# Seven-product weight sums with other signs, and two of them made by one 1024-column instruction

## The chip, the cores and the metric

The kernel runs on one core of a Trainium2 chip. The core has TensorE (matmuls; the profile lists its weight loads apart, as PEld), VectorE (DVE), ScalarE (ACT), GpSimd (POOL) and SyncE (SP), which here issues the loads and stores. The metric is the device time of one execution in microseconds (us); several executions are made, and their median is given.

## The reference, cut to what matters

One layer of a block on 256 tokens of width 4096, in float32:

```python
xn = rms_norm(h, norm_in_g[i])
proj = xn @ w_in[i]
q, k, v, z_a, a_c, g_c, z_c = split(proj)
y_a = chunked_attention(q, k, v, rel_table[i])
y_a = rms_norm(y_a, attn_out_g[i]) * silu(z_a)
y_c = conv_module(a_c, g_c, ...)
y_c = rms_norm(y_c, conv_out_g[i]) * silu(z_c)
h = h + concatenate([y_a, y_c]) @ w_out[i]
gate = sigmoid(rms_norm(h, ple_norm_g[i]) @ w_ple_gate[i] + b_ple_gate[i])
h = h + gate * (p[i] @ w_ple[i])
return rms_norm(h, final_g)
```

Nearly all of the work is products of 256 rows with large weight matrices: `w_in` (4096 x 14336), `w_out` and `w_ple_gate` (4096 x 4096 each), `w_pw` (2048 x 2048) and `w_ple` (256 x 4096).

## The kernel before

**Products in parts.** Each float32 operand is split into a high part (a cast to the matmul's rounded float32) and a low part (the operand less the high part). A product then takes three matmuls: high by high, low by high and high by low. ScalarE casts a weight tile `wt` to its high part `wh` (`prepare`, line 304), VectorE subtracts it to get the low part `wl` (`minus`, line 321). A weight tile is 128 rows by 1024 columns (512 KB), loaded by SyncE's queue.

**Seven products for eight.** Most of the large products run as `mixed_product`. It makes a 2 x 2 arrangement of output blocks, two halves h of 128 tokens by two groups j of 512 columns, each in a PSUM bank of its own. It walks over pairs of 128-row blocks of the weights. A pair has four weight blocks w00, w01 (first row block, column group 0 and 1, in the tile `w0`) and w10, w11 (second row block, in the tile `w1`). A plain pair takes eight block products, 24 matmuls. A seven-product pair takes seven, 21 matmuls, in Strassen's manner: P1 to P7, some of them with sums of the token blocks (`s_of`, made ahead) and with sums of the weight blocks. P1, P5, P6 and P7 add up in four extra PSUM banks (`acc_P` in the profile). After the last seven-product pair `on_helpers` adds these to the blocks (`helper_sums`). The orders in which plain and seven-product pairs follow each other are written out by hand (`steady`, `dense`, `delayed`, `early`, `late`; a star marks a seven-product pair; `early` has six). There are 117 such pairs in the kernel.

**What a seven-product pair does around its matmuls.** The high parts `h0` (w00 alone) and `h1` (w10, w11) are there already when the pair begins, since `prepare` makes them a unit ahead. VectorE then makes, in this order: the low part `l0` of w00 (512 columns, line 321); the sum w00 + w01 into the first half of `w0` (line 324); the low part `l1` of w10 and w11 (1024 columns, line 321); w01 + w11 into the second half of `w0`; then w00 + w01 + w11 into the second half of `w1` and that plus w10 into its first half. ScalarE casts the two sums in `w0` to `ah` (line 486) and the two in `w1` to `bh` (line 489). Then follow `prepare` for the next unit, work from the queue `later` (`fill`), and VectorE's low parts `al` and `bl` (line 321). The matmuls (line 446) use `h0`, `l0` in P1, `h1`, `l1` in P2 and P3, `ah`, `al` in P5 and P7, `bh`, `bl` in P6 and P4, in the order P1, P2, P3, P5, P7, P6, P4.

**What sets the order.** The weights' casts, sums and low parts are chained: on each engine they keep the order in which the code makes them (`chain`). What is not chained (matmuls, block ends, transposes and their splits, the attention and the layer norm) is placed among them by the framework's scheduler when the program is built; each engine then runs its list in order. Five weight tiles and five tiles each of high and low parts go round, so the engines ahead of TensorE can lead it by a few units and no more.

**The stages**, in order of time: the first product and its transposes; four rounds of a gate/convolution product and a query/key product (both with seven-product pairs) and a value product (plain, line 255, `product`), with attention and the convolution's taps filled in between; a layer norm of the convolution's result; the product with `w_pw` (plain, from about 901 us); the products for the two output gates, with `w_out` and with `w_ple_gate` (all with seven-product pairs); two last column groups in plain products, and the closing norm.

Of the kernel before, what the change touches and what calls it, by code (L numbers as in the profile page):

```python
# [16 lines left out]
P = 128  # L17
NB = 512
# [13 lines left out]
def hybrid_block(  # L32
# [290 lines left out]
    def plus(out, a, b):  # L323
        return chain(nc.vector.tensor_tensor(out, a, b, ALU.add))  # L324

    def product(w, col, lhs, kblocks, pool=None, tag="acc", ahead=None, lag=(), begun=None, fills=2):

        acc = begun or [  # L330
            (pool or ps_acc).tile([P, NB], F32, tag=tag, name=f"acc{h}") for h in range(NH)
        ]
        starts = range(FIRST if begun else 0, kblocks, KC)
        kept = list(starts[len(starts) - len(lag) :]) if lag else []
        held = []
        for k0 in starts:
            kc = min(KC, kblocks - k0)
            keep = k0 in kept
            if lag:
                wh, wl = weight_parts(w, col, k0, kc, lag[kept.index(k0)] if keep else None)  # L340
            else:
                (wt,), (wh,) = take(w, col, None, k0, "one")
                wl = part("wl")
                minus(wl, wt, wh)
                prepare()
            if keep:
                held.append((k0, kc, wh, wl))
            for k in range(kc):
                for h in range(1 if keep else NH):
                    accumulate(acc[h], h, lhs, k0 + k, wh, wl, k, kblocks)  # L350
                if ahead and begun and k0 + k == FIRST:
                    ahead(k0)
            if ahead:
                ahead(k0 + kc)
            fill(fills)

        def rest():
            for k0, kc, wh, wl in held:
                for k in range(kc):
                    accumulate(acc[1], 1, lhs, k0 + k, wh, wl, k, kblocks)  # L360

        return (acc, rest) if lag else acc
# [63 lines left out]

    def mixed_product(
        w, col, lhs, comb, order, on_helpers, ahead=None, fills=0, on_begin=None, apart=NB
    ):

        c = [[ps_acc.tile([P, NB], F32, tag="acc", name=f"acc{h}{j}") for j in range(2)] for h in range(NH)]
        helper = {}
        begun, ends = set(), {}
        for n, (_, seven) in enumerate(order):
            for name in ("P1", "P5", "P6", "P7", "P2", "P3", "P4") if seven else ("P2", "P3", "P4", "X"):
                ends[name] = n
        banks = {"P2": c[0][0], "P3": c[0][1], "P4": c[1][0], "X": c[1][1]}
        made = []  # L440

        def add(name, x, w2, n, final):

            for kind, (a, b) in enumerate(((x[0], w2[0]), (x[1], w2[0]), (x[0], w2[1]))):
                made.append(
                    nc.tensor.matmul(  # L446
                        banks[name], a, b, start=name not in begun,
                        stop=final and ends[name] == n and kind == 2,
                    )
                )  # L450
                begun.add(name)

        def block(kb, h):
            t = lhs[kb // 4]
            return [t[:, kb % 4, q, h * P : (h + 1) * P] for q in range(2)]

        last_seven = max((n for n, (_, seven) in enumerate(order) if seven), default=None)
        for n, (pair, seven) in enumerate(order):
            if ahead:
                ahead(pair)  # L460
            (w0, w1), (h0, h1) = take(w, col, apart, pair, "seven" if seven else "pair")
            l0, l1 = part("wl"), part("wl")
            if not seven:
                for wt, wh, wl in ((w0, h0, l0), (w1, h1, l1)):
                    minus(wl, wt, wh)
                prepare()
                fill(fills[0] if isinstance(fills, tuple) else fills)
                parts = ((h0, l0), (h1, l1))
                places = [(k, j, h) for k in range(2) for j in range(2) for h in range(NH)]
                if n in (0, len(order) - 1):  # L470
                    places = [(k, j, h) for j in range(2) for h in range(NH) for k in range(2)]
                for k, j, h in places:
                    name = (("P2", "P3"), ("P4", "X"))[h][j]
                    add(name, block(2 * pair + k, h), [t[:, j] for t in parts[k]], n, k == 1)
                continue
            begins = not helper
            if begins:
                for name in ("P1", "P5", "P7", "P6"):
                    helper[name] = ps_tmp.tile([P, NB], F32, tag="tmp", name=f"acc_{name}")
                banks.update(helper)  # L480
            minus(l0[:, :1], w0[:, :1], h0[:, :1])
            plus(w0[:, 0], w0[:, 0], w0[:, 1])
            minus(l1, w1, h1)
            plus(w0[:, 1], w0[:, 1], w1[:, 1])
            ah, bh = part("wh"), part("wh")
            chain(nc.scalar.copy(ah, w0))  # L486
            plus(w1[:, 1], w0[:, 0], w1[:, 1])
            plus(w1[:, 0], w1[:, 1], w1[:, 0])
            chain(nc.scalar.copy(bh, w1))  # L489
            prepare()  # L490
            fill(fills[1] if isinstance(fills, tuple) else fills)
            al, bl = part("wl"), part("wl")
            minus(al, w0, ah)
            minus(bl, w1, bh)
            first = len(made)

            def s_of(i):
                t, at = comb[pair // 4], pair % 4
                return [t[:, at + i // 2, q, (i % 2) * P : (i % 2 + 1) * P] for q in range(2)]

            k0, k1 = 2 * pair, 2 * pair + 1
            add("P1", block(k0, 0), (h0[:, 0], l0[:, 0]), n, True)
            add("P2", block(k1, 0), (h1[:, 0], l1[:, 0]), n, True)
            add("P3", s_of(3), (h1[:, 1], l1[:, 1]), n, True)
            add("P5", s_of(1), (ah[:, 0], al[:, 0]), n, True)
            add("P7", s_of(0), (ah[:, 1], al[:, 1]), n, True)
            add("P6", s_of(2), (bh[:, 1], bl[:, 1]), n, True)
            add("P4", block(k1, 1), (bh[:, 0], bl[:, 0]), n, True)
            if begins and on_begin:
                on_begin()  # L510
            if begins:
                tc.add_manual_dep(
                    made[first].ins, last_transpose[0].ins.name,
                    mybir.DependencyInfo(mybir.DependencyClass.NoSync, mybir.DependencyReason.DATA),
                    reason="transposes before the helpers take their banks",
                )
            if n == last_seven:
                on_helpers(helper)
        return c
# [4 lines left out]
    def helper_sums(helper, z):  # L524


        nc.scalar.copy(z[1][0], helper["P1"])
        tt(z[1][0], helper["P6"], z[1][0], ALU.add)
        tt(z[0][1], helper["P5"], z[1][0], ALU.add)
        tt(z[1][0], helper["P7"], z[1][0], ALU.add)  # L530
        tt(z[1][1], helper["P5"], z[1][0], ALU.add)

    def sum_tiles():
# [4 lines left out]
    def scaled_pair(w, col, apart, order, r, fills):  # L538
# [11 lines left out]
        def finals():  # L550
            for h, j in QUARTERS:
                stt(
                    z[h][j], c[h][j], r[:, h : h + 1], z[h][j],
                    ALU.mult, ALU.subtract if j else ALU.add,
                )

        closing.append(finals)
# [480 lines left out]
    def gated(ys, c0, col, r_y, order):  # L1038
# [7 lines left out]
        acc = mixed_product(w_in0, col + c0 * NB, xT, xS, order, on_helpers, fills=2)  # L1046
        for h, j in QUARTERS:
            zz, y = z[h][j], ys[c0 + j][:, h, :]
            tt(zz, acc[h][j], zz, ALU.subtract if j else ALU.add)
            nc.scalar.activation(zz, zz, AF.Silu, scale=r_x[:, h : h + 1])  # L1050
            later.append(partial(stt, y, y, r_y[:, h : h + 1], zz, ALU.mult, ALU.mult))

# [16 lines left out]
    for c0 in range(0, D // NB, 2):  # L1069
# [8 lines left out]
        def on_helpers(helper):  # L1078
# [1 line left out]
            h00, h01, h10, h11 = (hs[c0 + j][:, h, :] for h in range(NH) for j in range(2))  # L1080
            tt(h00, helper["P1"], h00, ALU.add)
            helper_sums(helper, z)
            tt(h01, h01, z[0][1], ALU.subtract)
            tt(h10, h10, z[1][0], ALU.add)
            tt(h11, h11, z[1][1], ALU.subtract)

        acc = mixed_product(
            w_out0, c0 * NB, yT, yS, dense if c0 else late, on_helpers,
# [54 lines left out]
    def gated_pair(c0, order, ahead):  # L1143
# [7 lines left out]
        def on_helpers(helper):  # L1151
            stt(z[0][0], helper["P1"], r_h[:, :1], rows[0], ALU.mult, ALU.add)
            helper_sums(helper, z)
            for h, j in QUARTERS[1:]:
                zz = z[h][j]
                stt(
                    zz, zz, r_h[:, h : h + 1], rows[j],
                    ALU.mult, ALU.subtract if j else ALU.add,
                )
            fgs.extend(broadcast_row(final_g, (c0 + j) * NB, NB) for j in range(2))  # L1160

# [8 lines left out]
        todo = []  # L1170
        for h, j in QUARTERS:
            gt, hc = z[h][j], hs[c0 + j][:, h, :]
            stt(gt, acc[h][j], r_h[:, h : h + 1], gt, ALU.mult, ALU.subtract if j else ALU.add)
            nc.scalar.activation(gt, gt, AF.Sigmoid)
            later.append(partial(tt, gt, pacc[j][h], gt, ALU.mult))
            todo.append(partial(tt, hc, hc, gt, ALU.add))
# [59 lines left out]
```

## Time and profile before

| what | value |
|---|---|
| median of 3 runs | 2048.63 us (2048.56 to 2048.75) |
| the profiled execution | 2046.57 us |
| its span, first to last instruction | 2044.8 us |
| granted TensorE clock, mean | 0.996 of full speed |
| ScalarE busy | 1370.8 us (67%) |
| DMA | 412.31 MB, mean 202 GB/s |

The span is what the profile sees of an execution; the profiled execution's own time is 1.8 us longer. Busy times are sums over an engine's instructions. "Idle before" counts the time an engine stood before an instruction, put down to what ended the wait. An `x` before a number is a count.

### The profile page before, as it was taken

Reading aid. Unit: us, or ns where it says so; the run is one execution under the profiler, and the core shown is the slowest. Engines: PE = TensorE matmul, PEld = TensorE weight load, DVE = VectorE, ACT = ScalarE, POOL = GpSimd, SP = SyncE. Lnnn points to the kernel's source line nnn. Section 1 sums busy time; section 2 is a strip of 40 time slices with the busy share of each in tenths; the row PEclk is TensorE's granted clock in tenths of the full one; section 3 lists DMA queues with packets and bytes.
Section 4 is the critical chain, followed back from the end, with each engine's and each line's share of the span. In section 5 each row is a group of like instructions: output and inputs, shape, how many; then the busy total and the mean of one; then the engine's idle time right before and its main releaser. Section 6 shows DMA issues by size and latency. Waiting matters only on the chain.

```text
span 2044.8 us, 26229 instructions
## 1 busy us (share of the span) xinstructions
PE 2018.8 (99%) x9103; PEld 1667.0 (82%) x9103; DVE 1816.4 (89%) x2241; ACT 1370.8 (67%) x2033; POOL 14.7 (1%) x23
## 2 busy tenths in 40 slices
PE   9999999999999999999999999999999999999997
PEld 6888888888888888878888888888888888888886
DVE  7589998999799988975889999999999998999954
ACT  7477798778977797774555556675565675565543
POOL 0000000000000000000000000000000000000010
PEclk9999999999999999999999999999999999999999
DMA  8646665656566665646565665765656655666764
GB/s 302 189 163 207 191 211 170 213 194 206 166 201 200 195 196 175 216 159 210 174 224 173 210 207 197 239 226 199 209 196 216 208 194 188 211 226 202 233 221 144
DMA packets 170335, 412.31 MB, mean 202 GB/s; under 512 B 13006, under 2 KB 16222, under 8 KB 170202
## 3 DMA queue, kind: packets, MB, share of 16 engines
q1 hardware_dynamic: 169914, 410.11, 61.1%
q8 instruction: 71, 1.16, 0.2%
q14 instruction: 62, 0.51, 0.1%
q10 hardware_dynamic: 288, 0.52, 0.1%
HBM read 406.39 MB, written 4.19 MB: 201 GB/s over the span
## 4 chain that ended last, share of the span: by engine, by line
PE 95%; ACT 1%; DVE 1%; DMA 1%; issue 1%; ACTq 0%; POOLq 0%; POOL 0%; DVEq 0%
PE acc L446 56%; PE acc L255 22%; PE acc_P L446 15%; PE tmp_ps L179 1%; DMA wt<-in_w_in_dram 0%; DVE wl L321 0%; PE tmp_ps L886 0%; PE tmp_ps L922 0%; PE tmp_ps L944 0%; DMA wt<-in_w_out_dram 0%; ACT wh L304 0%; ACT big_t L852 0%; ACT junk L562 0%; DMA pin<-in_p_dram 0%; PE tmp_ps L134 0%
## 5 line engine op out<-in xcount | busy, mean ns | idle before, releaser
L321 DVE TENSOR_TENSOR wl<-wt,wh 128x1024 fp32r<-128x1024 f32 x961 | 1087.6, 1154 | 126.2 <-ACT wh L304 107.3
L446 PE MATMUL acc<-wh,big_t 128*128 128x512 f32 x3410 | 1052.4, 390 | 1.5 <-ACT big_t L165 0.9
L304 ACT CAST wh<-wt 128x1024 fp32r<-128x1024 f32 x727 | 697.3, 981 | 298.9 <-PE acc L446 87.8
L446 PEld LDWEIGHTS acc<-wh,big_t 128*128 128x128 f32 x3410 | 638.1, 188 | 134.3 <-ACT big_t L165 1.4
L446 PE MATMUL acc<-wl,big_t 128*128 128x512 f32 x1705 | 663.2, 389 | 0.4 <-DVE wl L321 0.4
L255 PE MATMUL acc<-wh,big_t 128*128 128x512 f32 x1248 | 393.4, 397 | 7.1 <-ACT wh L304 5.7
L446 PEld LDWEIGHTS acc<-wl,big_t 128*128 128x128 f32 x1705 | 319.9, 188 | 68.2 <-DVE wl L321 1.6
L324 DVE TENSOR_TENSOR wt<-wt 128x512 f32<-128x512 f32 x468 | 322.6, 689 | 11.3
L255 PEld LDWEIGHTS acc<-wh,big_t 128*128 128x128 f32 x1248 | 232.2, 189 | 56.3 <-ACT wh L304 6.5
L486 ACT CAST wh<-wt 128x1024 fp32r<-128x1024 f32 x117 | 123.3, 1054 | 211.1 <-DVE wt L324 189.2
L446 PE MATMUL acc_P<-wh,big_t 128*128 128x512 f32 x852 | 262.4, 390 | 1.0 <-ACT wh L489 1.0
L255 PE MATMUL acc<-wl,big_t 128*128 128x512 f32 x624 | 244.1, 392 | 0.1
L714 ACT ACTIVATE prod<-uT,dw 128x255 f32<-128x255 f32 (+14 forms) x480 | 201.0, 490 | 3.7 <-DVE cv L721 3.6
L446 PEld LDWEIGHTS acc_P<-wh,big_t 128*128 128x128 f32 x852 | 159.7, 188 | 34.5 <-ACT wh L489 1.5
L446 PE MATMUL acc_P<-wl,big_t 128*128 128x512 f32 x426 | 165.5, 390 | 0.0
L489 ACT CAST wh<-wt 128x1024 fp32r<-128x1024 f32 x117 | 123.3, 1054 | 56.1 <-DVE wt L324 41.2
L721 DVE TENSOR_TENSOR cv<-cv,prod 128x1020 f32<-128x1020 f32 (+14 forms) x120 | 138.5, 1154 | 20.3 <-ACT prod L714 20.2
L255 PEld LDWEIGHTS acc<-wl,big_t 128*128 128x128 f32 x624 | 117.3, 188 | 26.0 <-DVE wl L321 1.3
L446 PEld LDWEIGHTS acc_P<-wl,big_t 128*128 128x128 f32 x426 | 79.9, 188 | 17.0 <-DVE wl L321 0.5
L562 ACT ACTIVATE junk<-hc 128x512 bf16<-128x512 f32 x32 | 20.2, 630 | 22.6 <-DVE hc L216 8.7
L165 ACT ACTIVATE big_t<-tmp_ps,prm 128x256 fp32r<-128x256 f32 x64 | 27.6, 474 | 4.6 <-DVE big_t L166 4.5
L166 DVE SCALAR_TENSOR_TENSOR big_t<-tmp_ps,prm,big_t 128x256 fp32r<-128x256 f32 x64 | 28.7, 476 | 2.2 <-ACT big_t L165 2.2
(189 smaller groups left out, 908.0 us busy)
## 6 DMA issues: line engine op xcount, KB each, us to landing
wt<-in_w_in_dram SPq DMA_DIRECT2D x447, 512.0 KB, 4.5
wt<-in_w_out_dram SPq DMA_DIRECT2D x128, 512.0 KB, 4.7
wt<-in_w_ple_gate_dram SPq DMA_DIRECT2D x128, 512.0 KB, 4.5
wt<-in_w_pw_dram SPq DMA_DIRECT2D x32, 512.0 KB, 4.4
hc<-in_x_dram SPq DMA_DIRECT2D x8, 512.0 KB, 5.6
wt<-in_w_ple_dram SPq DMA_DIRECT2D x8, 512.0 KB, 4.7
out_dram<-hc SPq DMA_DIRECT2D x16, 256.0 KB, 2.7
xin<-in_x_dram SPq DMA_DIRECT2D x7, 512.0 KB, 8.6
```

What stands on the lines that cost most here:

```text
L165: nc.scalar.activation(hi, src, AF.Identity, scale=scale),
L166: nc.vector.scalar_tensor_tensor(lo, src, scale, hi.bitcast(F32), ALU.mult, ALU.subtract),
L179: nc.tensor.transpose(pt[:, i * T + h * P : i * T + (h + 1) * P], src[:, h, b * P : (b + 1) * P], ident,)
L255: nc.tensor.matmul(acc, a, b[:, k, :], start=kb == 0 and kind == 0, stop=kb == kblocks - 1 and kind == 2,)
L304: chain(nc.scalar.copy(highs[k][:, :n], wt[:, :n]))
L321: return chain(nc.vector.tensor_tensor(wl, wt, wh.bitcast(F32), ALU.subtract))
L324: return chain(nc.vector.tensor_tensor(out, a, b, ALU.add))
L446: nc.tensor.matmul(banks[name], a, b, start=name not in begun, stop=final and ends[name] == n and kind == 2,)
L486: chain(nc.scalar.copy(ah, w0))
L489: chain(nc.scalar.copy(bh, w1))
L714: chain(nc.scalar.activation(dst[:, i, : T - n], uT[:, i, : T - n], AF.Identity, scale=dw[:, b, TAPS - 1 - n : TAPS - n], bias=0.0 if n el ...
L721: chain(nc.vector.tensor_tensor(cv[:, :, n:], cv[:, :, n:], made[n][:, :, : T - n], ALU.add))
```

## The change

The sums of the weight blocks are taken with other signs, so that two of the four have one common term, and that term is repeated over both halves of a 1024-column subtract. The first sum is w01 + w11 (second half of `w0`), the second is that less w00 (first half of `w0`); then `l1` is made, which stood between the first two sums; then `w1` less the first half of `w0`, repeated, gives w10 - (w01 + w11 - w00) and w11 - (w01 + w11 - w00) = w00 - w01 in one instruction. The first half of `w0` now belongs to P6, and the second half of `w1` to P5, so P6 and P5 change places in the order of the matmuls. Signs follow in `helper_sums` and where the blocks are finished: additions in the place of some subtractions. The token sums are as they were.

```diff
+    def less(out, a, b):
+        return chain(nc.vector.tensor_tensor(out, a, b, ALU.subtract))
...
             minus(l0[:, :1], w0[:, :1], h0[:, :1])
-            plus(w0[:, 0], w0[:, 0], w0[:, 1])
-            minus(l1, w1, h1)
             plus(w0[:, 1], w0[:, 1], w1[:, 1])
+            less(w0[:, 0], w0[:, 1], w0[:, 0])
             ah, bh = part("wh"), part("wh")
             chain(nc.scalar.copy(ah, w0))
-            plus(w1[:, 1], w0[:, 0], w1[:, 1])
-            plus(w1[:, 0], w1[:, 1], w1[:, 0])
+            minus(l1, w1, h1)
+            less(w1, w1, w0[:, :1].to_broadcast([P, 2, NB]))
             chain(nc.scalar.copy(bh, w1))
...
-            add("P5", s_of(1), (ah[:, 0], al[:, 0]), n, True)
+            add("P6", s_of(2), (ah[:, 0], al[:, 0]), n, True)
             add("P7", s_of(0), (ah[:, 1], al[:, 1]), n, True)
-            add("P6", s_of(2), (bh[:, 1], bl[:, 1]), n, True)
+            add("P5", s_of(1), (bh[:, 1], bl[:, 1]), n, True)
             add("P4", block(k1, 1), (bh[:, 0], bl[:, 0]), n, True)
...
         nc.scalar.copy(z[1][0], helper["P1"])
-        tt(z[1][0], helper["P6"], z[1][0], ALU.add)
+        tt(z[1][0], z[1][0], helper["P6"], ALU.subtract)
         tt(z[0][1], helper["P5"], z[1][0], ALU.add)
-        tt(z[1][0], helper["P7"], z[1][0], ALU.add)
+        tt(z[1][0], z[1][0], helper["P7"], ALU.subtract)
         tt(z[1][1], helper["P5"], z[1][0], ALU.add)
...
-            tt(zz, acc[h][j], zz, ALU.subtract if j else ALU.add)
+            tt(zz, acc[h][j], zz, ALU.add)
...
-            stt(gt, acc[h][j], r_h[:, h : h + 1], gt, ALU.mult, ALU.subtract if j else ALU.add)
+            stt(gt, acc[h][j], r_h[:, h : h + 1], gt, ALU.mult, ALU.add)
```

The block ends that are left out here (in `scaled_pair`, in `gated_pair`'s `on_helpers` and after `w_out`) change in the same way.

More of the change, by code (lines that the diff above doesn't have):

```diff
@@ L553, in finals @@
                     z[h][j], c[h][j], r[:, h : h + 1], z[h][j],
-                    ALU.mult, ALU.subtract if j else ALU.add,
+                    ALU.mult, ALU.add,
                 )
@@ L1082, in on_helpers @@
             helper_sums(helper, z)
-            tt(h01, h01, z[0][1], ALU.subtract)
+            tt(h01, h01, z[0][1], ALU.add)
             tt(h10, h10, z[1][0], ALU.add)
-            tt(h11, h11, z[1][1], ALU.subtract)
+            tt(h11, h11, z[1][1], ALU.add)
         acc = mixed_product(
@@ L1157, in on_helpers @@
                     zz, zz, r_h[:, h : h + 1], rows[j],
-                    ALU.mult, ALU.subtract if j else ALU.add,
+                    ALU.mult, ALU.add,
                 )
```

## The prediction

> **What bounds the kernel now.** I read the page first: its span line, its busy shares and the engine line of the chain that ended last.
>
> ```profile
> span 2044.8 us, 26229 instructions
> PE 2018.8 (99%) x9103; PEld 1667.0 (82%) x9103; DVE 1816.4 (89%) x2241; ACT 1370.8 (67%) x2033; POOL 14.7 (1%) x23
> PE 95%; ACT 1%; DVE 1%; DMA 1%; issue 1%; ACTq 0%; POOLq 0%; POOL 0%; DVEq 0%
> ```
>
> TensorE is busy for 2018.8 of 2044.8 us and is 95% of the chain. The change takes no matmul away, so it can only win from the 26 us in which TensorE stands. The next view is the busy time by windows of 51 us (us; then PE, PEld, DVE, ACT, POOL; granted clock, DMA share, GB/s).
>
> ```profile
> 153.00:204.00 51.00, 51.00 (x227) 41.84 (x227) 50.44 (x58) 38.88 (x61) 0.00 (x0) 1.00 0.63 209
> 869.00:920.00 51.00, 46.31 (x215) 37.56 (x214) 39.39 (x81) 39.77 (x77) 2.30 (x2) 0.93 0.48 158
> 1278.00:1329.00 51.00, 50.20 (x229) 41.30 (x228) 49.63 (x61) 32.94 (x41) 0.00 (x0) 1.00 0.71 239
> 1636.00:1687.00 51.00, 50.31 (x242) 41.78 (x241) 48.93 (x84) 36.21 (x60) 0.69 (x1) 1.00 0.58 193
> 1687.00:1738.00 51.00, 49.75 (x235) 41.33 (x234) 44.74 (x67) 29.39 (x42) 0.00 (x0) 1.00 0.59 188
> 1738.00:1789.00 51.00, 49.96 (x221) 41.02 (x220) 50.52 (x63) 30.02 (x39) 0.00 (x0) 1.00 0.62 211
> 1994.00:2045.00 51.00, 37.45 (x166) 30.67 (x164) 21.85 (x29) 17.32 (x24) 1.30 (x3) 0.91 0.41 145
> sum 2045.00, PE 2018.76 PEld 1667.03 DVE 1816.39 ACT 1370.77 POOL 14.73; mean PE 50.47 PEld 41.68 DVE 45.41 ACT 34.27 POOL 0.37
> ```
>
> The idle time of 26.24 us lies in few places: 13.55 in the last window (the closing of the kernel, no seven-product pair in it), 4.69 around 904 us, and 0.80, 0.69, 1.25 and 1.04 where one weight matrix gives way to the next. A steady window such as 153 to 204 has none, although VectorE runs there at 50.44 of 51. VectorE is the engine with least room, but it keeps ahead of TensorE. Who waits for whom says the same (us in total, times, longest):
>
> ```profile
> ACT wh L486 <- DVE wt L324: 189.2, 100, 3.2
> DVE wl L321 <- ACT wh L304: 107.3, 101, 2.0
> PEld acc_P L446 <- ACT wh L489: 1.5, 1, 1.5
> PE acc_P L446 <- ACT wh L489: 1.0, 1, 1.0
> ```
>
> ScalarE waits long for the weight sums (L324), yet TensorE waits for a cast of them (L489) exactly once.
>
> **The change part by part.** The prices are in the groups of instructions, shapes kept apart (count, busy us, mean ns, idle before).
>
> ```profile
> L321 DVE TENSOR_TENSOR wl<-wt,wh 128x1024 fp32r<-128x1024 f32 x844 | 1011.9, 1219 | 120.2 <-ACT wh L304 101.4 <-ACT wh L489 11.5
> L324 DVE TENSOR_TENSOR wt<-wt 128x512 f32<-128x512 f32 x468 | 322.6, 689 | 11.3
> L528 DVE TENSOR_TENSOR z<-acc_P,z 128x512 f32<-128x512 f32 x18 | 12.3, 682 | 0.8 <-PE acc_P L446 0.8
> L552 DVE SCALAR_TENSOR_TENSOR z<-acc,r_x,z 128x512 f32<-128x512 f32 x28 | 20.0, 739 | 0.0
> L721 DVE TENSOR_TENSOR cv<-cv,prod 128x1020 f32<-128x1020 f32 x4 | 4.9, 1218 | 5.9 <-ACT prod L714 5.9
> ```
>
> Step 1, the sums: 468 adds are four for each of 117 seven-product pairs. Two of 689 ns go and one 1024-column subtract in place comes. An in-place f32 sum of 1020 columns (L721) takes 1218, a 1024-column difference (L321) 1219, so I take 1219. No row has an operand that repeats its columns; the bounds are 0.689 (a half-width instruction) and 2.44 (twice the full one), and the nearest rows speak for 1.219. The Trainium skill, "VectorE: DVE Perf Modes", section "Walkthrough: the 8-slice pipeline in each mode", says that f32 with any stride runs at one result a cycle of 0.96 GHz; by that alone an estimate is 1.07 us and a start, which would leave the sum as it is. Saved per pair: 2 x 0.689 - 1.219 = 0.16 us, in all 117 x 0.16 = 18.6 us of VectorE's 1816.4. Next to the 228 us in which VectorE idles already, that is more of what is there already: in a steady window it frees nothing, as TensorE shows no gap there. Were VectorE the engine that paces the pairs, the 18.6 us would count in full.
>
> Step 2, the order: the low half l1 (1024 columns, used from P2's third matmul) is now made after two narrow instructions and no longer after one. P6 takes the old place of P5 and P5 that of P6; both of their operands still come from the same two casts, the first cast (L486) now 1.2 us earlier, as no l1 stands between its sums. Whether l1 becomes late is read from its lead. A usual pair: VectorE's l1, and TensorE's first matmul that uses it:
>
> ```profile
> 154.67 1.22 DVE L321 TENSOR_TENSOR wl<-wt,wh 128x1024 fp32r<-128x1024 f32 x1
> 159.84 0.39 PE L446 MATMUL acc<-wl,big_t 128*128 128x512 f32 x1
> ```
>
> That is 159.84 - 155.89 = 3.95 us of lead. I followed all 117 pairs in this way; the one with least lead is also the one whose cast TensorE waits for. Its VectorE rows, its two casts and its matmuls (start, us, engine, line):
>
> ```profile
> 1774.31 0.68 DVE L321 TENSOR_TENSOR wl<-wt,wh 128x512 fp32r<-128x512 f32 x1
> 1774.91 0.68 DVE L216 TENSOR_TENSOR hc<-hc,z 128x512 f32<-128x512 f32 x1
> 1775.51 0.68 DVE L324 TENSOR_TENSOR wt<-wt 128x512 f32<-128x512 f32 x1
> 1776.11 1.22 DVE L321 TENSOR_TENSOR wl<-wt,wh 128x1024 fp32r<-128x1024 f32 x1
> ...
> 1777.25 0.68 DVE L324 TENSOR_TENSOR wt<-wt 128x512 f32<-128x512 f32 x1
> ...
> 1778.45 0.68 DVE L324 TENSOR_TENSOR wt<-wt 128x512 f32<-128x512 f32 x1
> ...
> 1779.65 0.68 DVE L324 TENSOR_TENSOR wt<-wt 128x512 f32<-128x512 f32 x1
> ```
>
> ```profile
> 1778.02 1.05 ACT L486 CAST wh<-wt 128x1024 fp32r<-128x1024 f32 x1 [1.61 <-PE acc_P L446]
> 1780.43 1.05 ACT L489 CAST wh<-wt 128x1024 fp32r<-128x1024 f32 x1 [1.35 <-DVE wt L324]
> ```
>
> ```profile
> 1778.51 0.39 PE L446 MATMUL acc<-wl,big_t 128*128 128x512 f32 x1
> 1779.41 1.07 PE L446 MATMUL acc_P<-wh,big_t 128*128 128x512 f32 x4
> 1781.53 0.50 PE L446 MATMUL acc_P<-wh,big_t 128*128 128x512 f32 x1 [1.04 <-ACT wh L489]
> ```
>
> Here l1 ends at 1777.33 and is used at 1778.51: 1.18 us. One narrow instruction more in front of it costs a start distance of 0.60 (1774.31 to 1774.91, and 1775.51 to 1776.11). 0.58 remain, so l1 isn't late even here, and nowhere else.
>
> Step 3, what the stall at 1780 gives back. The four matmuls from 1779.41 last 1.07 us together and 0.39 alone, so they start (1.07 - 0.39) / 3 = 0.227 apart; the fifth is due at 1780.32 and starts at 1781.53: 1.21 us late, for the cast at 1780.43, for the add at 1779.65. Between the pair's sums VectorE did four adds of a finished block, which hang on no order. If those stay where they are, the sums end 0.16 earlier here and 0.16 earlier through the pair ahead of it, say 0.3; if they fall behind the shorter row of sums, the whole 1.21 goes. I take 0.8. What is late next is TensorE itself. In the other joints the first operands wait for transposes and their split; those splits stand behind VectorE's sums of the last pairs, and I put 0.4 for all three of 0.80, 0.69 and 1.25 together (the last hangs on a load).
>
> Step 4, signs: the block ends change subtract to add at the same shape, and two of the four helper sums take the PSUM operand second. No row shows that place for this shape; 36 instructions between 0.68 (L528) and 0.74 (L552, the three-operand form at this width) are at most 2 us of VectorE, spread over 18 block ends and covered as above. I take nothing.
>
> Sum: -0.8 - 0.4 = -1.2 us. The profiled execution took 2046.57 us, 1.8 more than its span; it becomes 2045.4. The median of the runs, 2048.63, lies 2.06 above it, and moves alike to **2047.4**. This case's own range is 2046.4 to 2048.4.
>
> **The rivals.** (a) The gap at 904 shrinks. It is the one large piece of idle time that isn't at an end of the kernel.
>
> ```profile
> 903.84:908.77 4.93, 0.39 (x3) 0.00 (x1) 1.90 (x8) 4.93 (x17) 0.51 (x1) 0.76 0.00 0
> 908.77:913.20 4.43, 4.39 (x10) 2.99 (x11) 4.43 (x4) 3.73 (x4) 0.18 (x1) 0.50 0.87 264
> ```
>
> TensorE stands 4.5 us while ScalarE is full (4.93 of 4.93), and then runs at a granted clock of 0.50: 10 matmuls take 4.43 where 2.27 would do. The work in front is a layer norm that VectorE feeds, straight after a product with six seven-product pairs (the order `early`); those give it 6 x 0.16 = 1.0 us. Against it: in this stretch the layer norm's matmuls have fixed places among TensorE's units and ScalarE's queue is the full one, so earlier sums alone don't shorten it; the program's order must fall another way. If it does by one unit of the product that runs there, 12 matmuls of 0.227, then 2.7 us go, and the 2.2 of the half clock with them: 2047.4 - 4.9 = 2042.5. The Trainium skill, "TensorE: Matmul & The Clock Gate", section "Part 1: The HAM clock gate", gives an idle window of about 3.4 us as what drops the clock to half; the trace agrees as far as one gap can show, and by it a gap shortened to 2 us would keep the full clock. Chance 0.14.
>
> (b) Nothing is gained: the adds stay in front, l1 or the wide subtract eats the 0.16. 2048.6, chance 0.15.
>
> (c) Slower, by order: what isn't chained is put in place anew at build, and one cast or split lands behind a block's adds at a joint or at 904. A gap longer by one unit of 2.7 us, at most with another 2.2 us of half clock: from 2047.4 + 2.7 = 2050.1 to 2048.6 + 4.9 = 2053.5. The same rows as (a) speak for it, with no sign; the shorter row of sums speaks against. Chance 0.09.
>
> (d) Slower, by the repeated operand: if the wide subtract ran at half speed, 2.44 us, a pair would cost 1.06 more on VectorE. The room is read here, the windows view and the groups of the same stretch:
>
> ```profile
> 1380.00:1650.00 270.00, 270.00 (x1192) 223.13 (x1191) 262.43 (x304) 160.17 (x187) 0.00 (x0) 1.00 0.61 203
> L324 DVE TENSOR_TENSOR wt<-wt 128x512 f32<-128x512 f32 x108 | 74.5, 690 | 2.8
> ```
>
> 27 pairs (108 adds) share 7.57 us of room, 0.28 each. It decides from 1.38 + 0.28 = 1.66 us on; at 2.44 each pair lacks 0.78, and over the 117 that is near 91 us, less where VectorE has more room: about 2120. Chance 0.02.
>
> **How the numbers follow.** Forecast 0.60, (a) 0.14, (b) 0.15, (c) 0.09, (d) 0.02. About 0.2%, 4.1 us, is what a measurement of this kernel can tell from no change. Faster by more than that: nearly all of (a), and a small tail of the forecast, 0.15. Slower: (d) and the far half of (c), 0.07. Within: 0.78. The range takes in the forecast, (b), the nearer half of (a) and the start of (c): 2042.6 to 2050.4.
>
> **What would show it.** 351 narrow and wide sums at the places of the 468, 234 of them near 0.69 us and 117 near 1.22; VectorE's busy time near 1798 with TensorE's unchanged; ScalarE's wait for the weight sums (189.2) well down, its wait for TensorE up; no wait of TensorE on l1; the wait on L489 at 1780 shorter or gone. It is wrong if a wide subtract is over 1.66 us, if TensorE has a new gap in a steady window, or if the gap at 904 moves by more than 2 us.

## The result and the profile after

The changed kernel takes 2045.28 us (median of 20 runs, 2043.89 to 2046.99), the one before 2048.25 (20 runs, 2046.79 to 2050.67). The ratio is 0.9985, with a 95% interval of 0.9978 to 0.9992: about 3 us faster, between 1.6 and 4.5. That is two and a half times what was forecast, and less than 0.2%. The time lies inside the wide range with the rivals, but below the 2046.4 to 2048.4 that the prediction gave as this case's own.

The page of the changed kernel, its span, busy shares and the engine line of the chain that ended last:

```profile
span 2043.4 us, 26018 instructions
PE 2018.3 (99%) x9103; PEld 1668.4 (82%) x9103; DVE 1801.0 (88%) x2124; ACT 1373.3 (67%) x2033; POOL 14.7 (1%) x23
PE 95%; DVE 2%; ACT 1%; issue 1%; DMA 1%; ACTq 0%; POOLq 0%; POOL 0%; DVEq 0%
```

VectorE has 117 instructions less and 15.4 us less busy time (1816.4 to 1801.0), TensorE the same matmuls. The two profiled spans differ by only 1.4 us, not by 3; that is taken up below. The groups of VectorE's sums, shapes kept apart (count, busy us, mean ns, idle before), and one of the helper sums whose second operand now lies in PSUM:

```profile
L327 DVE TENSOR_TENSOR wt<-wt 128x1024 f32<-128x1024 f32 x117 | 143.3, 1225 | 3.7
L327 DVE TENSOR_TENSOR wt<-wt 128x512 f32<-128x512 f32 x117 | 80.9, 691 | 3.8
L324 DVE TENSOR_TENSOR wt<-wt 128x512 f32<-128x512 f32 x117 | 80.2, 685 | 0.2 <-DMA wt<-in_w_ple_gate_dram 0.2
L532 DVE TENSOR_TENSOR z<-z,acc_P 128x512 f32<-128x512 f32 x18 | 12.3, 681 | 0.0
```

The subtract with the repeated operand costs 1225 ns, next to 1219 for a 1024-column difference without repetition, so repeating costs next to nothing. Nor does the place of the PSUM operand matter (681 ns as second operand, 682 as first in the kernel before). Who waits for whom (us, times, longest):

```profile
ACT wh L491 <- DVE wt L327: 129.2, 97, 1.9
DVE wl L321 <- ACT wh L304: 119.4, 111, 2.1
ACT wh L488 <- DVE wt L327: 76.4, 96, 3.3
PEld acc_P L449 <- ACT wh L491: 0.7, 1, 0.7
PE acc_P L449 <- ACT wh L491: 0.3, 1, 0.3
```

ScalarE's wait for the first two sums falls from 189.2 to 76.4 us and that for the second two rises from 41.2 to 129.2. TensorE's one wait for a cast falls from 1.5 to 0.7. The windows of 51 us in the middle of the kernel in which the prediction found idle time (us; PE, PEld, DVE, ACT, POOL; clock, DMA share, GB/s):

```profile
869.00:920.00 51.00, 46.32 (x214) 37.52 (x214) 38.91 (x80) 39.62 (x77) 2.30 (x2) 0.93 0.49 156
1278.00:1329.00 51.00, 50.24 (x229) 41.33 (x228) 48.76 (x57) 33.05 (x40) 0.00 (x0) 1.00 0.69 238
1636.00:1687.00 51.00, 50.42 (x243) 42.01 (x242) 48.77 (x81) 36.54 (x60) 0.69 (x1) 1.00 0.59 189
1687.00:1738.00 51.00, 49.90 (x235) 41.49 (x234) 44.53 (x63) 29.07 (x42) 0.00 (x0) 1.00 0.60 191
1738.00:1789.00 51.00, 50.68 (x224) 41.68 (x223) 50.58 (x61) 30.58 (x40) 0.00 (x0) 1.00 0.64 211
```

TensorE's idle time goes from 0.80, 0.69, 1.25 and 1.04 us to 0.76, 0.58, 1.10 and 0.32 in the last four; around 904 it stays (4.69, now 4.68). The pair at 1775 us, VectorE's rows and then the matmul that waits for the second cast:

```profile
1773.74 0.69 DVE L321 TENSOR_TENSOR wl<-wt,wh 128x512 fp32r<-128x512 f32 x1
1774.34 0.70 DVE L324 TENSOR_TENSOR wt<-wt 128x512 f32<-128x512 f32 x1
1774.94 0.70 DVE L216 TENSOR_TENSOR hc<-hc,row 128x512 f32<-128x512 f32 x1
1775.55 0.70 DVE L327 TENSOR_TENSOR wt<-wt 128x512 f32<-128x512 f32 x1
1776.15 1.23 DVE L321 TENSOR_TENSOR wl<-wt,wh 128x1024 fp32r<-128x1024 f32 x1
1777.28 0.70 DVE L216 TENSOR_TENSOR hc<-hc,z 128x512 f32<-128x512 f32 x1
1777.88 1.23 DVE L327 TENSOR_TENSOR wt<-wt 128x1024 f32<-128x1024 f32 x1
```

```profile
1778.92 1.07 PE L449 MATMUL acc_P<-wh,big_t 128*128 128x512 f32 x4
1780.31 0.73 PE L449 MATMUL acc_P<-wh,big_t 128*128 128x512 f32 x2 [0.32 <-ACT wh L491]
```

Due at 1778.92 + 4 x 0.227 = 1779.83, it starts at 1780.31: 0.48 us late where it was 1.21. Between l0 and the last sum stand two adds of a finished block (L216) where there were three (at 1774.91, 1777.85 and 1779.05); the row has one instruction less to put them between.

### The profile page after: what moved, and what is told of

It reads as the page before. It is cut to its first block, busy times and chain, and to the rows that moved or that the text cites. A ratio compares the mean times of both kernels' runs of the same rounds, so it can differ in the third digit from the quotient of the medians.

```text
span 2043.4 us, 26018 instructions
## 1 busy us (share of the span) xinstructions
PE 2018.3 (99%) x9103; PEld 1668.4 (82%) x9103; DVE 1801.0 (88%) x2124; ACT 1373.3 (67%) x2033; POOL 14.7 (1%) x23
## 4 chain that ended last, share of the span: by engine, by line
PE 95%; DVE 2%; ACT 1%; issue 1%; DMA 1%; ACTq 0%; POOLq 0%; POOL 0%; DVEq 0%
PE acc L449 55%; PE acc L255 22%; PE acc_P L449 15%; DVE wl L321 1%; PE tmp_ps L179 1%; DMA wt<-in_w_in_dram 0%; PE tmp_ps L888 0%; PE tmp_ps L924 0%; PE tmp_ps L946 0%; ACT big_t L854 0%; ACT wh L304 0%; ACT junk L564 0%; PE tmp_ps L134 0%; DMA pin<-in_p_dram 0%; PE tmp_ps L923 0%
## 5 line engine op out<-in xcount | busy, mean ns | idle before, releaser
L327 DVE TENSOR_TENSOR wt<-wt 128x512 f32<-128x512 f32 x234 | 224.2, 958 | 7.5
L491 ACT CAST wh<-wt 128x1024 fp32r<-128x1024 f32 x117 | 123.3, 1054 | 158.1 <-DVE wt L327 129.2
L488 ACT CAST wh<-wt 128x1024 fp32r<-128x1024 f32 x117 | 123.3, 1054 | 81.5 <-DVE wt L327 76.4
L324 DVE TENSOR_TENSOR wt<-wt 128x512 f32<-128x512 f32 x117 | 80.2, 685 | 0.2 <-DMA wt<-in_w_ple_gate_dram 0.2
```

What stands on the lines that cost most here:

```text
L327: return chain(nc.vector.tensor_tensor(out, a, b, ALU.subtract))
```

## The experiments

The theory was that VectorE's shorter row of sums shortens the few waits that TensorE has for it. What needed a test: the 1.6 us that the first two profiles don't show; whether the moved l1 or the shorter row gives the gain; and whether it is the width of the instruction.

**Both kernels once more.** Neither kernel is edited.

> The kernel before, profiled once more, for the 1.6 us of the 3.0 us between the medians that the two first profiles don't show. If the first profile of before was a lucky execution, this one's span is 2045.5 to 2047.5, and the added time lies in longer TensorE gaps at places that can be named. If the profiles are typical and the rest of the gain lies outside the span, the span is 2044.5 to 2045.0 again and the time around it is about 3 us here and 1.8 in the changed kernel.

> The changed kernel, profiled once more beside the one before. Theory (shorter row of sums at the joints): 0.9985 of the time before again; the matmul that waits for the second cast at 1780 us is 0.4 to 0.6 us late where it was 1.2, the gap at 904 is 4.9 as before. If the gap at 904 or its half clock makes the difference, it is this gap that differs between the two kernels in this pair of profiles, by 1 us or more.

The kernel before took 2048.15 us (11 runs; ratio to its own other runs 0.9998, 0.9989 to 1.0006), its profiled span is 2047.5 where the first was 2044.8. The changed one took 2045.49 (11 runs; 0.9981, 0.9972 to 0.9990), with a span of 2043.3 where the first was 2043.4. So the first profile of before was a lucky execution: its 2046.57 us are below the fastest of the 20 runs. The second, at 2049.31, is 1.2 above its own median, so the truth lies between the two. Of the 2.7 us between them, 1.4 are half clock behind the gap at 904 (below), and 1.7 lie between 917 and 1707 us: about 1.0 in waits of TensorE for low parts, most of them those of the sums, and 0.4 at the joint near 1327. The first profile of before:

```profile
PEld acc_P L446 <- DVE wl L321: 0.5, 2, 0.3
```

and the second one, with one of the waits from its timeline:

```profile
PEld acc_P L446 <- DVE wl L321: 1.8, 5, 0.6
```

```profile
1276.06 0.61 PE L446 MATMUL acc_P<-wh,big_t 128*128 128x512 f32 x2
1276.87 0.50 PE L446 MATMUL acc_P<-wl,big_t 128*128 128x512 f32 x1 [0.20 <-DVE wl L321]
```

This one lies in the middle of a product, in a window that the first profile showed without a gap. Two seven-product pairs follow each other there, and al and bl are ready little before TensorE needs them. In this execution a cast ahead of them stood 1.56 us for its weight load where it had stood 1.31, VectorE waited 0.28 and 0.20 us for casts, and al came late; why is not shown. Weight loads (PEld) run beside the matmuls (82% busy beside 99%), so such a wait is not all lost; the 1.0 us above is counted by the starts of the matmuls. In the first profile of the changed kernel the group is 0.2 us, once, and in the second it is not there. At 904 TensorE's matmuls start 4.92 to 4.93 us apart in every profile but that of the last experiment. Behind it TensorE loses between 2.0 and 3.8 us at the half clock (the time to the 25th matmul after the gap, less 24 x 0.227), whichever kernel runs (2.4 and 3.8 in the two profiles of before, 2.7 and 2.9 in those of the changed one), so about a microsecond of any single comparison is that. Between the second profiles it is 0.9 of 4.2 us, just under the 1 us that was to speak for the half clock as the cause.

**The place of l1 alone.** The sums of before with l1 after the first two, as the change has it:

```diff
             plus(w0[:, 0], w0[:, 0], w0[:, 1])
-            minus(l1, w1, h1)
             plus(w0[:, 1], w0[:, 1], w1[:, 1])
             ah, bh = part("wh"), part("wh")
             chain(nc.scalar.copy(ah, w0))
+            minus(l1, w1, h1)
```

> The kernel before with one thing moved: the low part l1 after the first two sums, as in the change; the four narrow sums and the signs are those of before. Theory (the time comes from VectorE's shorter row of sums): VectorE's busy time stays at 1816, and the time stays at that of before, within 0.7 us. Rival (the place of l1 gives the gain, the first cast being 1.2 us earlier): 2 to 3 us faster than before. Third (l1 late): slower by 0.5 us or more, with TensorE waiting on line 321.

2051.68 us (11 runs), 1.0012 (1.0003 to 1.0021): 2.7 us slower than the 2049.01 of before. The rival fell, and the theory's own numbers too: the instructions are the same, yet the time isn't, and VectorE's busy time is 1824.0 and not 1816. The third came true in its size but not in its cause: TensorE's waits on line 321 in the middle of products are for al, as in the kernel before (2.1 us in five places, where the second profile of before has 1.8 in five), and none is for l1.

**The change without that move.** The changed kernel with l1 back between the first two sums:

```diff
             plus(w0[:, 1], w0[:, 1], w1[:, 1])
+            minus(l1, w1, h1)
             less(w0[:, 0], w0[:, 1], w0[:, 0])
             ah, bh = part("wh"), part("wh")
             chain(nc.scalar.copy(ah, w0))
-            minus(l1, w1, h1)
             less(w1, w1, w0[:, :1].to_broadcast([P, 2, NB]))
```

> The changed kernel with l1 put back between the two first sums, where it was before; signs and the wide subtract stay. Theory: the shorter row alone does it, 0.9985 of before, within 0.5 us of the changed kernel. Rival (the place of l1 gives it): back to within 0.7 us of before.

> The version with l1 between the first two sums once more. If it is faster than the changed kernel, 0.9970 to 0.9980 of before, 1 to 2 us under the changed kernel's 2045.4, with the stall at 1780 gone. If the first result was the chip's scatter, 0.9980 to 0.9987.

2043.84 us (8 runs; 0.9974, 0.9964 to 0.9984) and 2044.23 (11 runs; 0.9981, 0.9972 to 0.9989), against 2045.28 and 2045.49 of the changed kernel. The first of the two was taken beside the changed kernel's 2045.49, and is 1.65 us lower. The second was taken beside a kernel before of 2047.94 and not 2049.01; its ratio is that of the changed kernel, and lies in the range that was to mean scatter. The stall at 1780 is gone in both profiles, as expected if the version is faster. So it is likely that the move costs time in this kernel, but the times alone don't show it; the table at the end of this section has more on it. The reason is in VectorE's timeline of one pair near 153 us. First the kernel before (its second profile), from l0 to al:

```profile
153.02 0.68 DVE L321 TENSOR_TENSOR wl<-wt,wh 128x512 fp32r<-128x512 f32 x1
153.74 0.69 DVE L324 TENSOR_TENSOR wt<-wt 128x512 f32<-128x512 f32 x1
154.35 1.22 DVE L321 TENSOR_TENSOR wl<-wt,wh 128x1024 fp32r<-128x1024 f32 x1
155.49 2.14 DVE L324 TENSOR_TENSOR wt<-wt 128x512 f32<-128x512 f32 x3
157.54 4.77 DVE L321 TENSOR_TENSOR wl<-wt,wh 128x1024 fp32r<-128x1024 f32 x4
```

the same with l1 moved:

```profile
154.49 0.68 DVE L321 TENSOR_TENSOR wl<-wt,wh 128x512 fp32r<-128x512 f32 x1
155.20 1.42 DVE L324 TENSOR_TENSOR wt<-wt 128x512 f32<-128x512 f32 x2
156.54 1.22 DVE L321 TENSOR_TENSOR wl<-wt,wh 128x1024 fp32r<-128x1024 f32 x1
157.79 1.42 DVE L324 TENSOR_TENSOR wt<-wt 128x512 f32<-128x512 f32 x2
159.12 4.77 DVE L321 TENSOR_TENSOR wl<-wt,wh 128x1024 fp32r<-128x1024 f32 x4
```

the changed kernel (second profile):

```profile
153.32 0.69 DVE L321 TENSOR_TENSOR wl<-wt,wh 128x512 fp32r<-128x512 f32 x1
153.92 0.69 DVE L324 TENSOR_TENSOR wt<-wt 128x512 f32<-128x512 f32 x1
154.64 0.69 DVE L327 TENSOR_TENSOR wt<-wt 128x512 f32<-128x512 f32 x1
155.25 1.22 DVE L321 TENSOR_TENSOR wl<-wt,wh 128x1024 fp32r<-128x1024 f32 x1
156.50 1.23 DVE L327 TENSOR_TENSOR wt<-wt 128x1024 f32<-128x1024 f32 x1
157.65 4.85 DVE L321 TENSOR_TENSOR wl<-wt,wh 128x1024 fp32r<-128x1024 f32 x4
```

and the changed kernel with l1 back:

```profile
153.55 0.68 DVE L321 TENSOR_TENSOR wl<-wt,wh 128x512 fp32r<-128x512 f32 x1
154.15 0.69 DVE L324 TENSOR_TENSOR wt<-wt 128x512 f32<-128x512 f32 x1
154.75 1.22 DVE L321 TENSOR_TENSOR wl<-wt,wh 128x1024 fp32r<-128x1024 f32 x1
155.89 1.95 DVE L327 TENSOR_TENSOR wt<-wt 128x512 f32<-128x512 f32 x2
157.77 4.96 DVE L321 TENSOR_TENSOR wl<-wt,wh 128x1024 fp32r<-128x1024 f32 x4
```

(In the last one a row joins the 512-column difference and the 1024-column one.) Read the distances from start to start, not the durations. In the kernel before, the first sum overwrites the half of `w0` that l0 has just read, and starts 0.72 after it; in the changed kernel it writes the other half and starts 0.60 after it. The wide subtract overwrites what l1 has just read and starts 1.25 after l1; with l1 back, it is the narrow difference that follows l1, which touches nothing of it, and starts 1.14 after it. A VectorE instruction that reads what the one right in front of it has written, or overwrites what that one has read, starts 0.11 to 0.12 us later. In the trace these carry a wait for VectorE's own semaphore. That wait alone is not the delay: the sum behind l1 in the kernel before carries it too, for an instruction further back, and starts 1.14 after l1. The kernel before has three such neighbours in a pair, with l1 moved it has four, the changed kernel has two and with l1 back one. From l0's start to al's start that makes 4.52, 4.63, 4.33 and 4.22 us, in the same order as the times. The pair is a usual one: over the 90 to 107 pairs of each profile with nothing else in the row, the medians are 4.52, 4.64, 4.33 and 4.22.

**The width.** The wide subtract as two narrow ones, all else as in the changed kernel:

```diff
-            less(w1, w1, w0[:, :1].to_broadcast([P, 2, NB]))
+            less(w1[:, 0], w1[:, 0], w0[:, 0])
+            less(w1[:, 1], w1[:, 1], w0[:, 0])
```

> The changed kernel with its 1024-column subtract made as two 512-column subtracts, so four narrow sums as before, with the new signs and order. VectorE's busy time goes back to about 1816 us. If the width is what saves (the prediction's count by durations, 0.16 us a pair), the time goes back to that of before, within 0.7 us. If it is the start distances (0.60 us from one narrow instruction to the next, 0.72 where the second one touches what the first one has just read or written), the row from the first low part to al is 0.60 + 0.72 + 0.61 + 1.25 + 0.60 + 0.61 = 4.39 us a pair here, 4.33 in the changed kernel and 4.52 in the one before, and the time is within 1.2 us of the changed kernel, 1.5 us or more faster than before.

2045.85 us (11 runs), 0.9989 (0.9980 to 0.9998); 4.40 us a pair from l0 to al in its timeline (153.79 to 158.19; 4.39 was expected from the start distances), busy time 1808.2 where 1816 was expected (rows that overlap count once in it). By ratio it is 0.8 to 1.6 us behind the changed kernel (0.9985 and 0.9981), with intervals that overlap, and faster than the kernel before by an interval that ends just short of no change. So most of the gain, by the medians, is there with the same four narrow instructions as before, and the signs leave fewer neighbours that wait for each other; the size of each part is not shown. The swap of P5 and P6 and the signs at the block ends, which this version has too, were not run alone.

**Less and more VectorE work.** The wide subtract left out, and the first low part made twice:

```diff
-            less(w1, w1, w0[:, :1].to_broadcast([P, 2, NB]))
```

> The changed kernel with the 1024-column subtract left out: P5 and P4 take w11 and w10 as they are, so the sums are not those of the reference. 117 x 1.14 us less on VectorE. Theory (VectorE's time counts only through the waits of TensorE that it still causes): at most 3 us faster than the changed kernel, near 2042 to 2043, with the gap at 904 and the joints at 1326, 1663 and 1702 left. Rival (VectorE paces the pairs): tens of us faster.

```diff
             minus(l0[:, :1], w0[:, :1], h0[:, :1])
+            minus(l0[:, :1], w0[:, :1], h0[:, :1])
```

> The changed kernel with the first low part (512 columns) of every seven-product pair made twice: 0.60 to 0.72 us more on VectorE a pair, which is 0.4 to 0.5 more than before had. Theory (a lead that is used up a little in every pair and then becomes stalls): 10 to 30 us slower than before, with TensorE waiting on lines 321 and 491 in many pairs. Rival (the time hangs on a few joints only, whatever VectorE does between them): less than 4 us slower than before.

Without the subtract VectorE is busy for 1667.1 us, 134 less, and the kernel takes 2044.77 (10 runs; 0.9983, 0.9974 to 0.9992): half a microsecond less than the changed one, by ratio the same, and no less than the version with l1 back. It was expected near 2042 to 2043. TensorE has no gap at 1780 any more, as with l1 back. Nor has it one at the joint near 1702, in either version: there the build placed the transposes of `p`, which wait for a load (1.10 us in the changed kernel), behind five matmuls of the next product. The joint near 1664 has grown from 0.58 to 1.45 us (1.43 with l1 back) and that near 1326 from 0.76 to 1.08, why is open; the gap at 904 remains. That is the floor on this side. On the other side the cover ends at once: 0.72 us more a pair (5.05 from l0 to al) gives 2085.54 us (4 runs; 1.018, 1.0164 to 1.0195), 40 more than the changed kernel, more than expected. Its waits:

```profile
PEld acc_P L449 <- ACT wh L492: 16.7, 17, 1.6
PE acc_P L449 <- ACT wh L492: 9.9, 14, 1.2
```

The wait that stood once in the kernel before now stands 17 times. Half of the 117 x 0.72 = 84 us shows up in the time; the kernel before stood close to this edge, and 0.11 us more a pair, as with l1 moved, already cost 2.7 us.

The table has the length of the row and the times side by side. The last column takes the half clock out of the profiled executions: the time from the first matmul of line 446 (449) to the last one in front of the gap at 904, plus that from the 25th matmul behind the gap to the last of line 446 (449). In the run with l0 twice the gap has moved, so it has none.

| kernel | l0 to al, median, us | neighbours that wait | ratio to before | without the gap and half clock, us |
|---|---|---|---|---|
| l0 twice | 5.05 | 3 | 1.018 | |
| before, l1 moved | 4.64 | 4 | 1.0012 | 1820.6 |
| before | 4.52 | 3 | 1 | 1815.6 and 1817.3 |
| changed, two narrow subtracts | 4.40 | 2 | 0.9989 | 1814.6 |
| changed | 4.33 | 2 | 0.9985 and 0.9981 | 1813.6 and 1813.3 |
| changed, l1 back | 4.22 | 1 | 0.9974 and 0.9981 | 1812.6 and 1812.6 |
| changed, no wide subtract | 3.21 | 1 | 0.9983 | 1813.0 |

By the last column the row's length and the time have one order down to the floor. The wide subtract is worth 1.1 to 1.4 us in it, putting l1 back 0.6 to 1.0, and the change as a whole 2.0 to 4.0. These are one or two executions each, and in the last two rows the new place of the transposes at 1702 has its share, so what the row's length alone gives there is not shown.

## Why the prediction was right or wrong

- **TensorE bounds, and VectorE's saving is mostly covered**: right. 15.4 us less VectorE time gave 3 us, and 134 us less than that gave 3.2 in all.
- **Step 1, "in a steady window it frees nothing, as TensorE shows no gap there"**: wrong, and with it the size. One execution was read as the kernel. Its steady windows were free of gaps, but in some pairs al and bl had no lead to spare: TensorE's weight loads waited for them in two places in the first profile of before and in five in the second. The prediction looked at the lead of l1 in all pairs and at that of al and bl only where TensorE already stood.
- **Step 1, the price of 0.16 us a pair by durations**: nearly the right number (4.52 - 4.33 = 0.19) for the wrong reason. The durations were as taken (0.69 and 1.22), but overlapping instructions are paced by their start distances; two instead of three neighbours that wait for each other make 0.12 of it, as the two narrow subtracts show (4.40).
- **Step 2, l1 isn't late**: right for TensorE, which has no new wait on it. But the move was counted as free on VectorE, and it puts l1 right in front of an instruction that overwrites its operand: 4.33 against 4.22 us a pair, and by the table's last column 0.6 to 1.0 us of the kernel at most.
- **Step 3, 0.8 us from the stall at 1780 and 0.4 from the joints**: right in place and size. In the first pair of profiles 1.21 - 0.48 = 0.73 us went there, and the idle time of the joint windows fell by 0.04, 0.11 and 0.15 us, 0.3 in all. These 1.0 us are what the prediction saw. The rest of the 3 us lies in the waits that step 1 put at nothing, and in joints that differ from one execution to the next.
- **Step 4, signs and operand places at nothing**: right for their durations (681 ns). That the signs change which neighbours touch each other was not seen.
- **Rivals**: (a) fell, the gap at 904 is the same in every profile of the two kernels; (b) and (c) did not come, though the edit to before with l1 moved shows a loss of the size that (c) gave, by a longer row and not by a longer gap at 904; (d) fell with the 1225 ns. What the prediction says beside (a), that a gap shortened to 2 us would keep the full clock, is not borne out: with l0 twice, TensorE stood idle for 2.55, 1.86 and 2.73 us at 191, 638 and 924 us, and within 1.4 us of the end of each the granted clock fell to 0.50 for 3.41 us. After 1.87 us at 415 it stayed full.

## What to carry to other kernels

An engine that feeds the bounding one with a small lead isn't covered because one profile shows no gap: read the lead of every operand, and read a second execution's profile, before a saving there is priced at nothing. Order a row of VectorE instructions so that none reads or overwrites what its neighbour has just touched; count the row from start to start. When several experiments change the same row, list its length beside the times: here the order of the one was the order of the other, down to the floor. And where one gap costs a varying stretch of half clock, leave that stretch out before two profiles are compared.

## What the runs showed of the hardware that was not expected

A VectorE instruction of 512 columns that touches nothing of its neighbour starts 0.60 us after it, although it lasts 0.69; one that must wait for its neighbour starts 0.72 after it. At 1024 columns it is 1.14 and 1.25. After the same gap at 904, with 4.5 us idle in it, TensorE lost between 2.0 and 3.8 us: the granted clock was 0.50 for 6.83 us in five profiles (the four of the two kernels, and the one without the wide subtract) and for 3.41 us in the other four. Idle stretches of 1.86 to 2.73 us were enough for 3.41 us of it in the run with l0 twice.
